# Four products of a Down step summed in one PSUM bank, with shared Mix banks and the Down weights' sums in Up block 1

## The chip, the cores and the metric

The kernel runs on one core of a Trainium2 chip. The metric is the device time of one execution, in microseconds (us). PE is the matmul engine (TensorE), DVE is VectorE, ACT is ScalarE, POOL is GpSimd, and SP issues the DMAs.

## What is computed

One encoder layer, applied with the same weights to two requests, 2048 and 1024 positions of 1024 channels. Both sub-layers have a residual sum around them:

```python
def _token_mixer(h, w_in, sgu_norm, w_spatial, b_spatial, w_out):
    z = h @ w_in                                     # 1024 x 1536
    f = fft2(z[..., :512] by groups of 128).real     # over positions x group channels
    zs = gelu(z[..., 512:]); u, v = zs[..., :512], zs[..., 512:]
    v = rmsnorm(v by heads of 128) * sgu_norm
    g = u * (w_spatial @ v in chunks of 128 positions + b_spatial)
    return concat([f, g]) @ w_out                    # 1024 x 1024

def _channel_mixer(h, w_up, conv_w, conv_b, w_down):
    a = conv3(h @ w_up) + conv_b                     # 1024 x 5632
    return (gelu(a[..., :2816]) * a[..., 2816:]) @ w_down

x = x + rmsnorm(_token_mixer(rmsnorm(x)));  x = x + rmsnorm(_channel_mixer(rmsnorm(x)))
```

## The kernel before

All data is fp32. An operand of a matmul is split into a rounded high part and the rest (`split`: a cast on ACT, then a subtraction on DVE, for some operands on POOL), and a product is high x high + high x low + low x high, three matmuls of 128x128 by 128x512 for each 128 rows of depth.

The large products go by Strassen-Winograd steps (`Step`): a 2x2 block product with seven products in place of eight. B11, B21, T4, T2, T3, T1, B22 are the numbers 0 to 6 of the products, and p0 to p6 are their PSUM banks, w0 to w6 their split left operands. `Step.sums` makes the four sums s1 to s4 of the left operand on POOL (s0 to s3 in the trace), `prep` splits one operand, `mm` runs the matmuls of one product into one bank, and `post` adds the bank to what the step has so far. In Down, `post` builds c11, c12, c21 and c22 from the seven banks in the half tiles u, c11, c21, c22, and `cadd` then adds these four to the partial result c that an earlier pass left in memory; `cload` fetches it and `cstore2` writes it back. A few steps at the end (`closing`) add straight into c.

The program is a sequence: Fourier, Gate (12 steps), Fourier again, Mix (12 mixes), Up in three blocks of 1024 positions (22 steps each, with the convolution in `centre` and `taps`, and the gate product in `gate`, on POOL), and Down in three passes q0, q1, q2 over the depth (12 steps each). Between stages `turnover` loads and splits the next right operands.

The order is written by hand: `at(slot, order, fn)` puts a call into a slot, and the slots are emitted in turn. A slot is one product. Each engine runs its instructions in the order emitted, and so does SP with the DMAs. `LEAD` says how many slots ahead of its product an operand is split (3 in Up, 2 elsewhere), and the second argument of `steps` how many slots ahead the sums stand. Pools: 43 tiles of 4 KB (`U`), 12 of 2 KB (`H`), 8 PSUM banks.

The right operand of Down needs sums of the weights too. `wd_load`, `wd_sums` and `wd_store` (four loads, four sums on POOL, four stores for each pair of blocks, eleven pairs) make them in the Gate stage and leave them in memory.

A mix makes rows of the mirrored halves: es (even) comes from one product, o (odd) from another, in two banks each; `odd_out` copies o to os on ACT, then POOL makes ds = es + os (L807) and es = es - os (L808). `direct` adds a product to ds from the d banks, `mirrored` one to es from the m banks (L887).

## Time and profile before

| | us |
|---|---|
| median of three runs | 2787.15 (2786.34 to 2789.84) |
| profiled execution | 2785.41 |
| its span | 2783.6 |
| PE busy | 2658.9 |
| DVE busy | 2254.6 |
| POOL busy | 1345.2 |
| ACT busy | 1192.9 |

The granted TensorE clock over the span is 0.987 of full speed. The stages start in the trace at: Gate 98.9, second Fourier 340, Mix 436, Up block 0 772.3, block 1 1236.3, block 2 1668.9, Down q0 2096.7, q1 2279.9, q2 2525.4; the last matmuls of Down are at 2766. A row of the timeline gives the start, the duration and, in square brackets, how long the engine had been idle and what ended that.

### The profile page before, as it was taken

Reading aid. Unit: us, or ns where it says so; the run is one execution under the profiler, and the core shown is the slowest. Engines: PE = TensorE matmul, PEld = TensorE weight load, DVE = VectorE, ACT = ScalarE, POOL = GpSimd, SP = SyncE. Lnnn points to the kernel's source line nnn. Section 1 sums busy time; section 2 is a strip of 40 time slices with the busy share of each in tenths; the row PEclk is TensorE's granted clock in tenths of the full one; section 3 lists DMA queues with packets and bytes.
Section 4 is the critical chain, followed back from the end, with each engine's and each line's share of the span. In section 5 each row is a group of like instructions: output and inputs, shape, how many; then the busy total and the mean of one; then the engine's idle time right before and its main releaser. Section 6 shows DMA issues by size and latency. Waiting matters only on the chain. (4 is left out here: it accounts for less than half of the span.)

```text
span 2783.6 us, 35169 instructions
## 1 busy us (share of the span) xinstructions
PE 2658.9 (96%) x11930; PEld 2161.3 (78%) x11930; DVE 2254.6 (81%) x3296; ACT 1192.9 (43%) x2273; POOL 1345.2 (48%) x866
## 2 busy tenths in 40 slices
PE   8899999999979999999999999999998999999997
PEld 7678887887757777777888887888886877887775
DVE  6788866767898888889887888888888677669998
ACT  5445534565544444454444444444443242214332
POOL 3856612548765545553122233212224356668787
PEclk9999999999999999999999999999999999999999
DMA  9446567667953454553443364344353465466665
GB/s 349 157 161 204 206 229 254 201 200 238 298 197 123 154 186 148 172 206 122 136 136 119 120 215 121 112 136 130 114 197 114 126 219 172 156 201 212 210 209 199
DMA packets 323924, 498.08 MB, mean 179 GB/s; under 512 B 27232, under 2 KB 176224, under 8 KB 323744
## 3 DMA queue, kind: packets, MB, share of 16 engines
q1 hardware_dynamic: 323744, 495.85, 54.0%
q8 instruction: 93, 1.52, 0.2%
q14 instruction: 87, 0.71, 0.1%
HBM read 337.42 MB, written 158.35 MB: 178 GB/s over the span
## 5 line engine op out<-in xcount | busy, mean ns | idle before, releaser
L1192 POOL TENSOR_TENSOR t0u<-t0u,t1u 128x1024 f32<-128x1024 f32 x66 | 178.7, 2710 | 410.9 <-ACT t0u L1191 232.5
L201 PE MATMUL p3u<-sox,w3u 128*128 128x512 f32 x792 | 197.4, 396 | 9.7 <-DVE w3u L101 6.6
L201 PE MATMUL p5u<-sox,w5u 128*128 128x512 f32 x792 | 193.4, 393 | 8.4 <-DVE w5u L101 8.4
L201 PE MATMUL p1u<-sox,w1u 128*128 128x512 f32 x792 | 194.6, 394 | 4.7 <-DVE w1u L101 3.4
L201 PE MATMUL p0u<-sox,w0u 128*128 128x512 f32 x792 | 191.8, 391 | 6.1 <-DVE w0u L101 5.7
L201 PE MATMUL p6u<-sox,w6u 128*128 128x512 f32 x792 | 192.8, 391 | 3.4 <-DVE w6u L101 3.4
L201 PE MATMUL p2u<-sox,w2u 128*128 128x512 f32 x792 | 193.1, 391 | 1.9 <-DVE w2u L101 1.7
L201 PE MATMUL p4u<-sox,w4u 128*128 128x512 f32 x792 | 190.5, 390 | 2.0 <-POOL w4u L101 1.9
L201 PEld LDWEIGHTS p3u<-sox,w3u 128*128 128x128 f32 x792 | 148.0, 190 | 48.9 <-DVE w3u L101 12.5
L201 PEld LDWEIGHTS p5u<-sox,w5u 128*128 128x128 f32 x792 | 148.8, 189 | 43.3 <-DVE w5u L101 12.4
L201 PEld LDWEIGHTS p1u<-sox,w1u 128*128 128x128 f32 x792 | 148.6, 189 | 41.2 <-DVE w1u L101 8.6
L201 PEld LDWEIGHTS p0u<-sox,w0u 128*128 128x128 f32 x792 | 148.0, 188 | 40.2 <-DVE w0u L101 9.0
L201 PEld LDWEIGHTS p6u<-sox,w6u 128*128 128x128 f32 x792 | 147.4, 188 | 39.0 <-DVE w6u L101 8.6
L201 PEld LDWEIGHTS p2u<-sox,w2u 128*128 128x128 f32 x792 | 147.6, 188 | 37.8 <-DVE w2u L101 7.5
L201 PEld LDWEIGHTS p4u<-sox,w4u 128*128 128x128 f32 x792 | 148.2, 188 | 35.1 <-POOL w4u L101 3.2
L1143 ACT ACTIVATE t1u<-p2u,cbt,cwt 128x512 f32<-128x512 f32 x66 | 51.5, 780 | 286.2 <-DVE p2u L1131 286.2
L209 ACT COPY ud<-p0d 128x512 f32<-128x512 f32 x34 | 20.0, 588 | 344.1 <-PE p0d L201 344.1
L1191 ACT ACTIVATE t0u<-t0u 128x1024 f32<-128x1024 f32 x66 | 70.1, 1062 | 201.9 <-DVE t0u L1155 138.9
L1143 ACT ACTIVATE t0u<-p1u,cbt,cwt 128x512 f32<-128x512 f32 x66 | 51.5, 781 | 234.5 <-DVE p1u L1137 234.5
L101 POOL TENSOR_TENSOR w4u<-a4u,w4u 128x512 fp32r<-128x512 f32 x44 | 56.9, 1295 | 192.3 <-ACT w4u L100 174.6
L1155 DVE SCALAR_TENSOR_TENSOR t0u<-p6u,cwt,t0u 128x511 f32<-128x511 f32 (+4 forms) x220 | 111.7, 533 | 6.0 <-ACT t0u L1143 2.0
L1155 DVE SCALAR_TENSOR_TENSOR t1u<-p2u,cwt,t1u 128x511 f32<-128x511 f32 (+4 forms) x220 | 111.7, 533 | 3.1
(363 smaller groups left out, 7268.5 us busy)
## 6 DMA issues: line engine op xcount, KB each, us to landing
g_d<-t0u SPq DMA_DIRECT2D x66, 512.0 KB, 2.9
srx<-xo_d SPq DMA_DIRECT2D x42, 512.0 KB, 6.3
xT<-xT SPq DMA_DIRECT2D x24, 512.0 KB, 8.5
xc<-xc SPq DMA_DIRECT2D x24, 512.0 KB, 5.5
zz<-z_d SPq DMA_DIRECT2D x48, 256.0 KB, 6.1
xr<-x_po SPq DMA_DIRECT2D x24, 512.0 KB, 5.5
xo_d<-hT SPq DMA_DIRECT2D x48, 256.0 KB, 4.0
ra0d<-g_d SPq DMA_DIRECT2D x24, 512.0 KB, 6.7
```

What stands on the lines that cost most here:

```text
L101: (eng or vec).tensor_tensor(l, src, h.bitcast(F32), op=ALU.subtract)
L201: nc.tensor.matmul(ps, lhsT=w[:, a, k], rhs=op[k][:, b], start=k == 0 and a + b == 0, stop=k == n - 1 and a == 1)
L209: nc.scalar.copy(self.u, p[0])
L1143: nc.scalar.activation(t[:, i], p, AF.Identity, bias=cbt[:, ti : ti + 1], scale=cwt[:, ti, 1:2])
L1155: vec.scalar_tensor_tensor(d, a, w, d, op0=ALU.mult, op1=ALU.add)
L1191: nc.scalar.activation(ga, ga, AF.Gelu_apprx_tanh)
L1192: nc.gpsimd.tensor_tensor(ga, ga, self.t[1], op=ALU.mult)
```

## The change

Down: the products go in the order B11, B21, T2, T1, T3, B22, T4. B11, T2, T3 and T4 run into one bank, each on top of what is there, and after each of them the bank is added to its quarter of c as it stands (in q0, where there is no c yet, it is copied by ACT). B21, T1 and B22 have banks of their own and are added too; T1's is added twice. The tile u and `cadd` are gone. c is loaded two slots ahead of the step; the sums stand three slots ahead. The weights' sum for T4 has the opposite sign.

Mix: odd and direct run into the same two banks. `odd_out` makes es - o on DVE straight from PSUM, and what was es becomes ds, to which the bank with odd and direct together is added after direct.

The weights' sums of Down, with their loads and stores, stand in Up block 1, one pair per step. In Up block 0 the operands are split two slots ahead (three as before in the other blocks), the sums stand three slots ahead, and the first two steps load one slot later. H has 14 tiles.

```diff
-    H = ctx.enter_context(tc.tile_pool(name="h", bufs=12))
+    H = ctx.enter_context(tc.tile_pool(name="h", bufs=14))
...
         def mm(self, j):
-            ps = self.p[j] = bank(f"p{j}{self.nm}")
+            chained = j in self.CHAIN[1:]
+            ps = self.p[j] = self.p[self.CHAIN[0]] if chained else bank(f"p{j}{self.nm}")
             w, op, n = self.w.pop(j), self.stage.op[j], self.n
             for k in range(n):
                 for a, b in ((0, 0), (0, 1), (1, 0)):
                     nc.tensor.matmul(
-                        ps, lhsT=w[:, a, k], rhs=op[k][:, b], start=k == 0 and a + b == 0, stop=k == n - 1 and a == 1
+                        ps, lhsT=w[:, a, k], rhs=op[k][:, b], start=k == 0 and a + b == 0 and not chained,
+                        stop=k == n - 1 and a == 1, skip_group_check=j in self.CHAIN,
                     )
...
     def wd_sums(i):
         t1 = half(f"wt{i}")
         bs = raws["wd", i]
-        right_sums(t1, *bs)
+        right_sums(t1, *bs, False)
+        nc.gpsimd.tensor_tensor(bs[2], bs[2], bs[0], op=ALU.subtract)
         bs.append(t1)
...
-    for i in range(NFT // 2):
-        at(SB + 7 * i + 1, LOAD, wd_load, i)
-        at(SB + 7 * i + 3, PREP, wd_sums, i)
-        at(SB + 7 * i + 7, STORE, wd_store, i)
...
         def odd_out(self):
-            os = unit(f"os{self.nm}", F32, (128, 2, 512))
-            self.ds = unit(f"ds{self.nm}", F32, (128, 2, 512))
+            self.ds = self.es
+            self.es = unit(f"em{self.nm}", F32, (128, 2, 512))
             for c in range(2):
-                nc.scalar.copy(os[:, c], self.o[c])
-            nc.gpsimd.tensor_tensor(self.ds, self.es, os, op=ALU.add)
-            nc.gpsimd.tensor_tensor(self.es, self.es, os, op=ALU.subtract)
+                vec.tensor_sub(self.es[:, c], self.ds[:, c], self.o[c])
...
         def direct(self):
-            self.m = [bank(f"d{c}{self.nm}") for c in range(2)]
-            product(*self.m, self.g[0], WG)
+            product(*self.o, self.g[0], WG, first=False, chain=True)
 
         def direct_out(self):
             for c in range(2):
-                vec.tensor_add(self.ds[:, c], self.ds[:, c], self.m[c])
+                vec.tensor_add(self.ds[:, c], self.ds[:, c], self.o[c])
...
     class Up(Step):
...
-        LEAD = 3
...
+            self.LEAD = 3 if blk else 2
...
+        if blk == 1:
+            for i in range(NFT // 2):
+                at(s + 7 * i + 22, LOAD, wd_load, i)
+                at(s + 7 * i + 25, PREP, wd_sums, i)
+                at(s + 7 * i + 29, STORE, wd_store, i)
...
-                at(u.s0 - 3, LOAD, u.load)
-                at(u.s0 - 3, PREP - 0.2, u.sums)
+                at(u.s0 - 2, LOAD, u.load)
+                at(u.s0 - 2, PREP - 0.2, u.sums)
                 products(u)
             elif blk == 0:
-                steps(u, 4)
+                steps(u, 3)
...
     class Down(Step):
+        ORDER = (B11, B21, T2, T1, T3, B22, T4)
+        CHAIN = (B11, T2, T3, T4)
...
         def cstore(self):
...
-                    nc.sync.dma_start(c_d[2 * self.tp + i, :, h], self.quads(i)[h])
+                    nc.sync.dma_start(c_d[2 * self.tp + i, :, h], self.c[i][h])
...
-        def cadd(self, i):
-            for h in range(2):
-                eng = vec if i == 0 and self.q == 2 else nc.gpsimd
-                eng.tensor_tensor(self.c[i][:, h], self.c[i][:, h], self.quads(i)[h], op=ALU.add)
-
         def post(self, j):
-
-            if not self.closing:
-                return super().post(j)
             p, add = self.p, vec.tensor_add
...
+            new = {B11: 0, T2: 1, T3: 3, T4: 2}.get(j)
+            if j == B11 and self.q == 0:
+                self.c = [[None, None], [None, None]]
+            if self.q == 0 and new is not None:
+                self.c[new // 2][new % 2] = half(f"c{new}{self.nm}")
+                nc.scalar.copy(self.c[new // 2][new % 2], p[j])
+            (c11, c12), (c21, c22) = self.c if self.q == 0 else ((c[:, 0], c[:, 1]) for c in self.c)
+            if self.q or new is None:
+                c = {B11: c11, B21: c11, T2: c12, T1: c12, B22: c12, T3: c22, T4: c21}[j]
+                add(c, c, p[j])
+            if j == T3:
+                add(c22, c22, p[T1])
...
-        turnover(s, stage, *(() if q else (range(7), 10, 14)))
+        turnover(s, stage, Down.ORDER, *(() if q else (10, 14)))
...
-            steps(d)
+            steps(d, 3)
...
-            at(s if d.closing else s + 3, LOAD, d.cload)
-            if not d.closing:
-                at(s + 6, OUT + 0.2, d.cadd, 1)
-                at(s + 7, OUT + 0.2, d.cadd, 0)
+            at(s - 2, LOAD, d.cload)
             if q == 1:
+                at(s + 8, STORE, d.cstore2, 0)
                 at(s + 8, STORE, d.cstore2, 1)
-                at(s + 9, STORE, d.cstore2, 0)
...
-                at(s + 4, OUT + 0.1, d.square, 1, 0)
-                at(s + 5, OUT + 0.1, d.square, 1, 1)
-                at(s + 6, OUT + 0.1, d.square, 0, 1)
+                at(s + 4, OUT + 0.1, d.square, 1, 1)
+                at(s + 5, OUT + 0.1, d.square, 0, 1)
+                at(s + 6, OUT + 0.1, d.square, 1, 0)
```

Where the rows of the order below have names such as s0g5 or w4u0_12, the digits behind the letter are the step (g5 is Gate step 5; u0_12 is Up block 0, step 12; d1_6 is Down q1, step 6).

POOL in the Gate stage, before, from step 4's last sum to step 5's first; wt and wd are the weights' sums, rvg the reciprocal root for the norm:

```order
L183 TENSOR_TENSOR s3g4_1554<-ra0g4_1431,s1g4_1552 128x512
L93 TENSOR_SCALAR rvg3_v_1639<-vsg3_1472 128x8
L94 TENSOR_TENSOR rvg3_y_1640<-rvg3_v_1639,power_84 128x8
L126 TENSOR_TENSOR wt4_1727<-wd41_1652,wd40_1651 128x512
L127 TENSOR_TENSOR wd41_1652<-wd43_1654,wd41_1652 128x512
L128 TENSOR_TENSOR wd40_1651<-wd41_1652,wd40_1651 128x512
L130 TENSOR_TENSOR wd42_1653<-wd40_1651,wd42_1653 128x512
L180 TENSOR_TENSOR s0g5_1767<-ra1g5_1648 128x512
```

and after:

```order
L184 TENSOR_TENSOR s3g4_1490<-ra0g4_1380,s1g4_1488 128x512
L93 TENSOR_SCALAR rvg3_v_1575<-vsg3_1413 128x8
L94 TENSOR_TENSOR rvg3_y_1576<-rvg3_v_1575,power_84 128x8
L181 TENSOR_TENSOR s0g5_1686<-ra1g5_1580 128x512
L182 TENSOR_TENSOR s1g5_1687<-s0g5_1686,ra0g5_1579 128x512
```

The four operations on wt and wd no longer stand between the root and s0 of the next step.

ACT in Up block 0, before, between the centres of step 11 and the casts of step 12:

```order
L1143 ACTIVATE t1u0_11_9234<-p2u0_11_9220,cbt_83,cwt_82 128x512
L1143 ACTIVATE t1u0_11_9234<-p5u0_11_9200,cbt_83,cwt_82 128x512
L1145 COPY halo_99<-p5u0_11_9200 128x1
L100 CAST w3u0_12_9240<-s1u0_12_9190 128x512
L100 CAST w4u0_12_9260<-s2u0_12_9191 128x512
L1143 ACTIVATE t0u0_11_9277<-p1u0_11_9263,cbt_83,cwt_82 128x512
L1143 ACTIVATE t0u0_11_9277<-p6u0_11_9243,cbt_83,cwt_82 128x512
L1145 COPY halo_99<-p6u0_11_9243 128x1
L100 CAST w5u0_12_9284<-s0u0_12_9189 128x512
```

and after:

```order
L1141 ACTIVATE t1u0_11_8984<-p2u0_11_8970,cbt_83,cwt_82 128x512
L1141 ACTIVATE t1u0_11_8984<-p5u0_11_8942,cbt_83,cwt_82 128x512
L1143 COPY halo_99<-p5u0_11_8942 128x1
L100 CAST w0u0_12_8990<-ra0u0_12_8892 128x512
L100 CAST w3u0_12_9010<-s1u0_12_8960 128x512
L1141 ACTIVATE t0u0_11_9027<-p1u0_11_9013,cbt_83,cwt_82 128x512
L1141 ACTIVATE t0u0_11_9027<-p6u0_11_8993,cbt_83,cwt_82 128x512
L1143 COPY halo_99<-p6u0_11_8993 128x1
L100 CAST w4u0_12_9034<-s2u0_12_8961 128x512
```

The cast of w4 moved from ahead of the centre of p1u to behind it, and the cast of w0 stands ahead of w3's.

DVE in Down q1, step 6, before:

```order
L101 TENSOR_TENSOR w3d1_6_20947<-s1d1_6_20877,w3d1_6_20947 128x512
L212 TENSOR_TENSOR c11d1_6_20963<-ud1_6_20939,p1d1_6_20950 128x512
L101 TENSOR_TENSOR w4d1_6_20966<-s2d1_6_20878,w4d1_6_20966 128x512
L101 TENSOR_TENSOR w5d1_6_20987<-s0d1_6_20876,w5d1_6_20987 128x512
L214 TENSOR_TENSOR ud1_6_20939<-ud1_6_20939,p3d1_6_20990 128x512
L101 TENSOR_TENSOR w6d1_6_21004<-s3d1_6_20879,w6d1_6_21004 128x512
L217 TENSOR_TENSOR c21d1_6_21020<-ud1_6_20939,p4d1_6_21007 128x512
L101 TENSOR_TENSOR w0d1_7_21030<-ra0d1_7_20943,w0d1_7_21030 128x512
L220 TENSOR_TENSOR c22d1_6_21046<-c21d1_6_21020,p5d1_6_21033 128x512
L221 TENSOR_TENSOR c21d1_6_21020<-c21d1_6_21020,p2d1_6_20969 128x512
L222 TENSOR_TENSOR ud1_6_20939<-ud1_6_20939,p5d1_6_21033 128x512
L101 TENSOR_TENSOR w1d1_7_21050<-ra0d1_7_20943,w1d1_7_21050 128x512
```

and after:

```order
L101 TENSOR_TENSOR w3d1_6_20767<-s1d1_6_20706,w3d1_6_20767 128x512
L1307 TENSOR_TENSOR c0d1_6_20730<-c0d1_6_20730,p0d1_6_20770 128x512
L101 TENSOR_TENSOR w5d1_6_20788<-s0d1_6_20705,w5d1_6_20788 128x512
L1307 TENSOR_TENSOR c0d1_6_20730<-c0d1_6_20730,p1d1_6_20791 128x512
L101 TENSOR_TENSOR w4d1_6_20807<-s2d1_6_20707,w4d1_6_20807 128x512
L1307 TENSOR_TENSOR c0d1_6_20730<-c0d1_6_20730,p0d1_6_20770 128x512
L101 TENSOR_TENSOR w6d1_6_20823<-s3d1_6_20708,w6d1_6_20823 128x512
L1307 TENSOR_TENSOR c0d1_6_20730<-c0d1_6_20730,p5d1_6_20826 128x512
L101 TENSOR_TENSOR w2d1_6_20848<-ra1d1_6_20650,w2d1_6_20848 128x512
L1307 TENSOR_TENSOR c1d1_6_20732<-c1d1_6_20732,p0d1_6_20770 128x512
L1309 TENSOR_TENSOR c1d1_6_20732<-c1d1_6_20732,p5d1_6_20826 128x512
```

Each step's additions all read a bank, and three of them name p0, the bank that four products share; the additions into u, c21 and c22 are gone.

## Rows read from the trace of the kernel before

**Rows 1.** The page's busy line: engine, us, share of the span, instructions.

```profile
PE 2658.9 (96%) x11930; PEld 2161.3 (78%) x11930; DVE 2254.6 (81%) x3296; ACT 1192.9 (43%) x2273; POOL 1345.2 (48%) x866
```

**Rows 2.** Busy time by stage: stretch, length, each engine's us, PEclk, DMA share, GB/s.

```profile
98.90:340.00 241.10, 226.12 (x1065) 186.33 (x1064) 198.50 (x287) 119.62 (x323) 155.90 (x120) 0.98 0.56 189
436.00:772.30 336.30, 319.96 (x1702) 268.52 (x1702) 239.12 (x302) 185.60 (x366) 192.32 (x116) 0.97 0.72 231
772.30:1236.30 464.00, 440.66 (x1873) 346.01 (x1872) 396.68 (x542) 207.55 (x395) 257.53 (x167) 0.99 0.51 169
1236.30:1668.90 432.60, 425.40 (x1861) 347.99 (x1860) 364.54 (x654) 191.65 (x316) 113.06 (x59) 1.00 0.43 140
1668.90:2096.70 427.80, 421.98 (x1838) 344.59 (x1836) 375.47 (x731) 191.00 (x314) 107.94 (x59) 1.00 0.42 136
2279.90:2525.40 245.50, 237.80 (x1030) 194.81 (x1029) 178.70 (x191) 69.35 (x132) 170.21 (x111) 0.99 0.59 192
2525.40:2766.00 240.60, 229.61 (x977) 182.20 (x977) 229.75 (x217) 80.73 (x147) 197.06 (x123) 0.99 0.63 202
```

**Rows 3.** Timeline of Up block 1, PE and POOL: start, us, engine, line, operation.

```profile
1418.33 2.88 PE L201 MATMUL p0u<-sox,w0u 128*128 128x512 f32 x12
...
1423.77 2.88 PE L201 MATMUL p4u<-sox,w4u 128*128 128x512 f32 x12
1417.24 1.29 POOL L101 TENSOR_TENSOR w4u<-a4u,w4u 128x512 fp32r<-128x512 f32 x1 [3.80 <-ACT w4u L100]
```

**Rows 4.** Timeline of a Gate step, POOL and DVE.

```profile
190.45 1.29 POOL L126 TENSOR_TENSOR wt<-wd,wd 128x512 f32<-128x512 f32 x1 [0.41 <-DMA wd<-wd]
...
196.47 1.34 POOL L180 TENSOR_TENSOR s0g<-ra1g 128x512 f32<-128x512 f32 x1
195.97 5.71 DVE L449 SCALAR_TENSOR_TENSOR v2g<-v2g,rvg_y,gsg 128x128 f32<-128x128 f32 x8
201.60 0.68 DVE L101 TENSOR_TENSOR w4g<-s2g,w4g 128x512 fp32r<-128x512 f32 x1
```

**Rows 5.** The norm's line in the Gate stage: duration in ns, min/median/max.

```profile
L449 DVE SCALAR_TENSOR_TENSOR v2g<-v2g,rvg_y,gsg x79: 336/341/1454, 126.5 to 339.9; 128x128 f32<-128x128 f32 x79
```

**Rows 6.** Groups, POOL in Down q1, then DVE in q2: xcount | busy us, mean ns.

```profile
L1290 POOL TENSOR_TENSOR c1d<-c1d,c22d 128x512 f32<-128x512 f32 x8 | 13.9, 1739 | 0.0
...
L1290 DVE TENSOR_TENSOR c0d<-c0d,c11d 128x512 f32<-128x512 f32 x9 | 16.0, 1775 | 0.0
```

**Rows 7.** Groups of the Mix stage, POOL and DVE.

```profile
L807 POOL TENSOR_TENSOR ds<-es,os 128x1024 f32<-128x1024 f32 x12 | 34.7, 2895 | 46.4 <-ACT os L806 43.7 <-ACT xr L911 2.0 <-issue 0.7
...
L808 POOL TENSOR_TENSOR es<-es,os 128x1024 f32<-128x1024 f32 x11 | 27.3, 2481 | 0.9
...
L887 DVE TENSOR_TENSOR es<-es,m 128x512 f32<-128x512 f32 x22 | 14.1, 681 | 8.1 <-POOL es L808 8.1
```

**Rows 8.** Groups of the Gate stage, POOL: the costliest of the weights' sums.

```profile
L127 POOL TENSOR_TENSOR wd<-wd,wd 128x512 f32<-128x512 f32 x11 | 19.1, 1733 | 0.9
```

**Rows 9.** Waits of PE, Gate stage: us in total, times, longest.

```profile
PE p4g L201 <- DVE w4g L101: 10.5, 10, 2.1
PE p4g L201 <- ACT w4g L100: 2.4, 1, 2.4
```

**Rows 10.** Waits of PE, Mix stage.

```profile
PE x L666 <- DVE ds L879: 5.9, 3, 3.0
PE pq L756 <- DVE tl L101: 4.2, 3, 3.3
PE pq L756 <- DVE ehl L101: 2.3, 1, 2.3
```

**Rows 11.** Timeline of a step of Up block 0: PE, DVE, ACT.

```profile
1112.55 2.88 PE L201 MATMUL p1u<-sox,w1u 128*128 128x512 f32 x12
1119.41 0.68 DVE L1137 TENSOR_TENSOR p1u<-uu,p1u 128x512 f32<-128x512 f32 x1
1120.13 0.78 ACT L1143 ACTIVATE t0u<-p1u,cbt,cwt 128x512 f32<-128x512 f32 x1 [2.89 <-DVE p1u L1137]
```

More of the change, by code (lines that the diff above doesn't have):

```diff
@@ L165, in tile_trunk @@
         LEAD = 2
+        CHAIN = ()
         def __init__(self, stage, nm):
@@ L656, in w4_split, with product @@
         W4.append(h)
-    def product(o0, o1, aparts, wparts, first=True, last=True):
+    def product(o0, o1, aparts, wparts, first=True, last=True, chain=False):
         n_last = len(aparts) - 1
@@ L665, in product @@
                 for c, o in ((0, o0), (1, o1)):
-                    nc.tensor.matmul(o, lhsT=a, rhs=w[:n, c * 512 : (c + 1) * 512], start=st, stop=sp)
+                    nc.tensor.matmul(
+                        o, lhsT=a, rhs=w[:n, c * 512 : (c + 1) * 512], start=st, stop=sp, skip_group_check=chain
+                    )
     OFFS = (0, 128, 260, 384)
@@ L799, in odd @@
             self.o = [bank(f"o{c}{self.nm}") for c in range(2)]
-            product(*self.o, self.Q, WQ)
+            product(*self.o, self.Q, WQ, chain=True)
         def odd_out(self):
-            os = unit(f"os{self.nm}", F32, (128, 2, 512))
-            self.ds = unit(f"ds{self.nm}", F32, (128, 2, 512))
+            self.ds = self.es
+            self.es = unit(f"em{self.nm}", F32, (128, 2, 512))
             for c in range(2):
-                nc.scalar.copy(os[:, c], self.o[c])
-            nc.gpsimd.tensor_tensor(self.ds, self.es, os, op=ALU.add)
-            nc.gpsimd.tensor_tensor(self.es, self.es, os, op=ALU.subtract)
+                vec.tensor_sub(self.es[:, c], self.ds[:, c], self.o[c])
             if self.special:
@@ L1285, in cload @@
                 self.c.append(c)
-        def cadd(self, i):
-            for h in range(2):
-                eng = vec if i == 0 and self.q == 2 else nc.gpsimd
-                eng.tensor_tensor(self.c[i][:, h], self.c[i][:, h], self.quads(i)[h], op=ALU.add)
         def post(self, j):
-            if not self.closing:
-                return super().post(j)
             p, add = self.p, vec.tensor_add
-            (c11, c12), (c21, c22) = ((c[:, 0], c[:, 1]) for c in self.c)
-            if j == 0:
-                self.u = half(f"u{self.nm}")
-                nc.scalar.copy(self.u, p[0])
-            elif j == 1:
-                add(c11, c11, p[1])
-                nc.gpsimd.tensor_tensor(c11, c11, self.u, op=ALU.add)
-            elif j == 2:
-                vec.tensor_sub(c21, c21, p[2])
-            elif j == 3:
-                add(self.u, self.u, p[3])
-                add(c12, c12, self.u)
-            elif j == 4:
-                add(self.u, self.u, p[4])
-                add(c21, c21, self.u)
-                add(c22, c22, self.u)
-            elif j == 5:
-                add(c22, c22, p[5])
-                add(c12, c12, p[5])
-            elif j == 6:
-                add(c12, c12, p[6])
+            new = {B11: 0, T2: 1, T3: 3, T4: 2}.get(j)
[10 more added lines that the diff above has]
+                add(c22, c22, p[T1])
         def cstore2(self, i):
```

## The prediction

> **What bounds the kernel now.** I read the page's busy line first, then the busy times by stage, then in each stage the waits of PE, and for each wait the timeline around one occurrence. The page [rows 1] has PE busy for 2658.9 us, 96% of the span. Since the change keeps every matmul, only PE's gaps can be won. The stages [rows 2] say where these lie. Products follow each other every 2.72 us (two of them from 1418.33 to 1423.77 in [rows 3]), so a step of seven takes 19.05 us. Up block 2 is 22 steps, 419 us at that pace, and takes 427.8; block 0 has as many steps and takes 464.0, 36 us more. Down q1 and q2 are 12 steps each, 228.6 us, and take 245.5 and 240.6. The Gate stage leaves PE idle for 241.1 - 226.1 = 15.0 us, the Mix stage for 336.3 - 320.0 = 16.3. What PE waits for is nearly always an operand that DVE splits; the question is who makes DVE late.
>
> One behaviour decides that. A 128x512 subtraction with both operands in SBUF takes DVE 0.68 us when POOL rests (w4g at 201.60 in [rows 4]), and the norm's 128x128 operation 0.341 us at the median [rows 5]; but the eight that start at 195.97 take 5.71 us beside POOL's sums, twice 8 x 0.341 [rows 4]. In Down q2 the sum of c11 into c0, two SBUF operands again, has a mean of 1.78 us [rows 6]. Operations that read PSUM stay at 0.68 (L887 in [rows 7]). So POOL's work costs DVE time, and where DVE is at its limit, PE time. The Trainium skill ("SBUF — State Buffer", section "Who interferes with whom") gives a reason: a DVE instruction with two SBUF inputs shares a read port with GpSimd, and whoever issues first shuts the other out. These rows agree.
>
> **Gate: the weights' sums leave.** In each of eleven steps POOL does four of them (four groups of eleven, the costliest with a mean of 1733 ns, [rows 8]) ahead of the step's own s0 to s3. In the step shown they hold POOL from 190.45 to 196.47; s0 to s2 then fall on the norm at 195.97, which ends near 201.6, and only then is w4g split [rows 4]. PE waits for that split 10.5 us in ten steps, and 2.4 for its cast [rows 9]. Without them s0 can start 6 us earlier and is past the norm's start; the norm shrinks by 5.71 - 2.73 = 3.0 us, three times the mean wait of 1.05. I take both rows, **-13**. At the small end the step's sums collide instead with the splits of w2g and w3g, and half is left, -7; at the large end all 15.0 of idle goes and the clock of 0.98 rises too, -18.
>
> **Mix: odd and direct share banks.** Removed are 24 ACT copies and two POOL operations of 1024 columns a mix, 34.7 and 27.3 us in all; added are 24 DVE subtractions from PSUM at L887's 0.68 us, 16.3 us [rows 7]. DVE gets back the 8.1 us in which L887 waited for POOL's es (L808), and is without POOL beside it for 62 us more. It is busy 239 of 336 us [rows 2], so it has room. PE's waits on DVE here are 5.9 + 4.2 + 2.3 = 12.4 us [rows 10], and that is the term, **-12**. Ends: -4 if the new subtractions stand just ahead of those splits, and -24 if all 16.3 of idle goes and most of what the clock's 0.97 costs. The o banks are held longer, through direct, and the d banks are free in return.
>
> **Up block 0: casts two products ahead, not three; sums three, not four.** In ACT's order w4's cast now stands behind the centre of p1u. The chain to the operand is then: DVE's operation on p1u 0.68 us, two centres of 0.78 on ACT, the cast (taken at a centre's price), and POOL's subtraction of 1.29 [rows 3, 11]: 4.3 us, with two products, 5.44, to do it in. 1.1 us are to spare if DVE takes p1u at once. In the step shown it doesn't: p1u's matmuls end at 1112.55 + 2.88 = 1115.43, DVE takes it at 1119.41 and ACT follows at 1120.13 [rows 11]. But that delay came in good part from the old order, in which w3's split waited behind the centre of p2u; with w0's cast ahead of w3's there DVE has other work. For the twenty steady steps I take **0**: +16 if 0.8 us a step of that delay is left, -10 if over half of what these steps lose now goes (of the 36 us against block 2 I give them 17, about half, and the start the rest). The start of the block, where the first pair's loads come a product later and POOL does less Mix work beside them, is **-1**, plus or minus 4.
>
> **Up block 1: the weights' sums arrive.** Each step gets 6 us of POOL (190.45 to 196.47, [rows 4]) in a stage where POOL is busy 113 of 432.6 us [rows 2]. They can delay w4u's subtraction, which ends at 1417.24 + 1.29 = 1418.53 and is needed at 1423.77 [rows 3]: 5.2 us hide most of it. DVE has 432.6 - 364.5 = 68 us idle in 22 steps, 3 a step, and loses about 1 of it beside the sums. I take **+2**, range 0 to +8. The eight transfers a step go to a stage where DMA is busy 0.43 of the time, from one where it is 0.56, and stand in SP's queue ahead of operand loads that are issued six products before their use; nothing for them.
>
> **Down: four products in one bank, results added from PSUM.** A step of q1 loses four POOL additions (1.74 us for c22, [rows 6]), one of q2 two on POOL and two on DVE, 1.78 and, by the uncontended price, 0.68. DVE's posts go from seven to eight, +0.68, each with an operand in PSUM, which contention doesn't lengthen. For DVE in q2 that is -1.8 us a step, where it is busy 229.8 of 240.6 us, the tightest of [rows 2]; in q1 it is the contention of four POOL additions less. The two stages stand 17 + 12 = 29 us over their steps; I take a third, **-9** (turnovers -5, steady q2 -3, closing -1). Large end two thirds, -18; small end +6, where the chain costs. The chain is a new wait: T2, T3 and T4 write a bank that DVE must have read since the chain's last product, with one other product, 2.72 us, between. Behind that addition in DVE's row stands the split that the next product needs anyway, so where DVE is late the wait adds one addition, 0.68 us, at most. The c loads are issued five products earlier, ahead of later operand loads on SP, and cover themselves.
>
> **The sum**, against the profiled execution's 2785.41 us: -13 - 12 - 1 + 0 + 2 - 9 = -33, 2752.4. The median of the runs stands 1.7 us above that execution, so the forecast is 2754.
>
> **Rivals.** 1, the other side: block 0's shorter lead. If DVE goes on taking p1u 4 us late, w4 comes 4.3 + 4.0 - 5.4 = 2.9 us late in each of 20 steps: 58 us, less the 17 lost there now, +41, giving 2795. It turns the result from 2.5 us a step on ((33 + 17) / 20); at half the delay it gives 2766. For it speaks the row at 1119.41, against it the new order of the casts and DVE's 464 - 397 = 67 idle us. 2, Mix gives nothing, because the 24 subtractions fall where DVE splits for PE: 2766. 3, the chain: in q2 DVE is so late that each step of q1 and q2 waits for the bank twice, 0.5 us each, over 24 steps +24, with the -9 kept: 2778. The Trainium skill speaks against reading a bank in use ("PSUM — Partial Sum Buffer", section "Summary: rules for kernel authors": while a result is read, matmuls should go to a different bank); here they do, through B21, T1 and B22 in between, and PE stands only if the read outlasts a product. No row of before shows such a wait. 4, the sums spoil block 1, w4u 1 us late in eleven steps: +11 in place of +2, 2763.
>
> **How the numbers follow.** Forecast 0.60; rival 1 0.16, half of it slower than before; rival 2 0.11; rival 3 0.08; rival 4 0.05. About 0.2%, 5.6 us, is what a measurement can tell from no change. Slower: 0.08 of rival 1, 0.02 of rival 3, 0.01 of several small ends together, 0.11. Same: 0.03 of rival 1 and 0.03 of rival 3, 0.06. Faster: 0.83. Below the forecast the terms' ends lie 5, 12, 4, 10, 2 and 9 us off, as independent errors 19; above it 6, 8, 4, 16, 6 and 15, 25. For 8 in 10 I go to 2728 below, and above to 2787, which takes in rivals 2, 3, 4 and the lower half of 1.
>
> **What would show it.** Right: in the Gate stage PE's waits for w4g sum to under 3 us; in Mix its waits for ds and tl are gone; POOL in q1 is down by some 70 us, and DVE in q2 by some 20; block 0 stays within 10 us of 464. Wrong: PE waiting for w4u or w3u in block 0 over 1 us a step; PE's waits in Down ended by DVE's additions into c (the chain); block 1 over 437 us with PE waiting for w4u.

## The result

The changed kernel takes 2759.05 us (2757.78 to 2759.55, four runs) where the kernel before takes 2788.24 in four runs: a ratio of 0.9895, 95% interval 0.9878 to 0.9912. The forecast was 2754, in a range of 2728 to 2787. The total is right; the terms of block 0 and block 1 lie outside their ranges, and Mix gave half of its term.

The page's busy line of the changed kernel, which answers to [rows 1], and its busy times by stage, which answer to [rows 2] (the same stages in the same order: Gate, Mix, Up block 0, 1 and 2, Down q1, q2):

```profile
PE 2650.9 (96%) x11930; PEld 2164.6 (78%) x11930; DVE 2156.4 (78%) x3282; ACT 1199.7 (44%) x2261; POOL 1172.1 (43%) x772
```

```profile
100.50:324.90 224.40, 221.64 (x1064) 186.15 (x1065) 164.59 (x289) 119.35 (x324) 91.63 (x76) 0.98 0.31 99
...
421.40:752.25 330.85, 317.92 (x1703) 267.51 (x1701) 244.51 (x330) 173.38 (x342) 134.54 (x95) 0.97 0.74 241
752.25:1205.55 453.30, 433.72 (x1873) 349.53 (x1872) 375.15 (x543) 207.76 (x395) 258.46 (x164) 0.98 0.52 172
1205.55:1653.40 447.85, 434.20 (x1861) 344.74 (x1859) 390.03 (x650) 191.73 (x316) 176.83 (x102) 1.00 0.56 185
1653.40:2085.05 431.65, 420.79 (x1837) 343.35 (x1837) 379.25 (x738) 191.01 (x314) 110.08 (x60) 1.00 0.41 133
...
2266.90:2514.80 247.90, 239.67 (x1029) 196.26 (x1030) 172.90 (x201) 71.82 (x123) 104.16 (x68) 0.97 0.57 190
2514.80:2742.00 227.20, 223.69 (x977) 184.09 (x977) 189.64 (x203) 75.57 (x130) 144.42 (x94) 0.99 0.65 209
```

Both programs issue the same 11930 matmuls, so the start of the n-th matmul in one trace can be set against the n-th in the other. The differences over a stage, in us, with the stage bounded by times of the kernel before:

| stretch | forecast | measured |
|---|---|---|
| Gate, 98.9 to 340 | -13 | -15.8 |
| second Fourier, 340 to 436 | 0 | +1.5 |
| Mix, 436 to 772.3 | -12 | -5.8 |
| block 0, start, to 840 | -1 | -0.9 |
| block 0, steady, to 1236.3 | 0 | -10.6 |
| block 1 with its turnover, to 1668.9 | +2 | +16.3 |
| block 2 and Down q0, to 2279.9 | 0 | 0.0 |
| Down q1, then q2, to 2766 | -9 | +3.4, -11.8 |
| last matmul | -33 | -24.1 |

The stretch before 98.9 gives another -0.5, and -1.9 behind the last matmul makes up the span's -26.0. Block 1 is 14 us worse than the sum had it, Mix 6 worse, block 0 11 better, the Gate stage 3 better.

**Block 1.** The steps with sums take 20.7 to 20.8 us between equal matmuls (ten of the eleven; the first takes 19.5), and the first without them is back at 19.04. A step of the changed kernel, PE, DVE and POOL:

```profile
1416.56 2.56 PE L203 MATMUL p3u<-sox,w3u 128*128 128x512 f32 x10 [0.50 <-DVE w3u L101]
...
1414.75 1.75 DVE L101 TENSOR_TENSOR w3u<-a3u,w3u 128x512 fp32r<-128x512 f32 x1 [2.08 <-ACT w3u L100]
...
1428.27 2.76 DVE L101 TENSOR_TENSOR w1u<-a1u,w1u 128x512 fp32r<-128x512 f32 x1
...
1414.66 1.30 POOL L694 TENSOR_TENSOR wd<-wd,wd 128x512 f32<-128x512 f32 x1
...
1428.09 2.40 POOL L1190 TENSOR_TENSOR t0u<-t0u,t1u 128x1024 f32<-128x1024 f32 x1 [10.43 <-ACT t0u L1189]
```

The split of w1u comes 0.18 us after the gate product has started on POOL and takes 2.76 us: until POOL's operation ends at 1430.49, and then another 0.54. The split of w3u comes 0.09 us after the start of the last weights' sum and takes 1.75 us, again until 0.54 behind the end of that operation (1415.96). How little DVE had to spare in the kernel before shows in the pace of its own steps; this split of w3u is followed by the next at 1435.01, 18.4 us later:

```profile
1416.62 0.69 DVE L101 TENSOR_TENSOR w3u<-a3u,w3u 128x512 fp32r<-128x512 f32 x1 [2.02 <-ACT w3u L100]
```

From 1320 to 1446 DVE keeps this pace there and never waits for PE, while a step of PE takes 19.04: the 0.6 us between the two are all its slack. (Once it has caught up, from 1448 on, it waits for PE.) The 2.02 us ahead of w3u are none: ACT's cast stands behind the centre of p2u, which stands behind DVE's own operation on p2u, so this gap moves with DVE. In that stretch the splits take 1.70 us (w0u) and 0.69 (w1u, w3u); in the changed kernel they take 0.68, 2.76 and 1.75, together 2.1 us more. DVE's step is 20.77 us there, 2.35 longer; less the slack of 0.62, that is the 1.73 us lost.

### The profile page after: what moved, and what is told of

The parts are those of the page before. It is cut to its first block, busy times and chain, and to the rows that moved or that the text cites. A ratio compares the mean times of both kernels' runs of the same rounds, so it can differ in the third digit from the quotient of the medians.

```text
span 2757.6 us, 35060 instructions
## 1 busy us (share of the span) xinstructions
PE 2650.9 (96%) x11930; PEld 2164.6 (78%) x11930; DVE 2156.4 (78%) x3282; ACT 1199.7 (44%) x2261; POOL 1172.1 (43%) x772
## 4 chain that ended last, share of the span: by engine, by line
PE 43%; DVE 7%; issue 3%; ACT 1%; DMA 1%; POOL 0%; SPq 0%; DVEq 0%; ACTq 0%; POOLq 0%
PE p0d L203 12%; PE p5u L203 4%; PE p4u L203 4%; PE p2u L203 4%; PE p3u L203 4%; PE p6d L203 3%; PE p0u L203 3%; PE p1d L203 3%; PE p5d L203 3%; PE p1u L203 3%; PE p6u L203 2%; DVE sow L156 1%; DVE w3u L101 1%; DVE t1u L1153 1%; DVE t0u L1153 1%
## 5 line engine op out<-in xcount | busy, mean ns | idle before, releaser
L203 PEld LDWEIGHTS p0u<-sox,w0u 128*128 128x128 f32 x792 | 149.1, 189 | 47.3 <-DVE w0u L101 16.3
L203 PEld LDWEIGHTS p6u<-sox,w6u 128*128 128x128 f32 x792 | 148.9, 188 | 33.9 <-DVE w6u L101 2.8
L181 POOL TENSOR_TENSOR s0d<-ra1d 128x512 f32<-128x512 f32 (+1 forms) x36 | 50.2, 1396 | 204.1 <-DMA ra1d<-g_d 190.1
L93 POOL TENSOR_SCALAR r_v<-ss 128x2 f32<-128x2 f32 (+1 forms) x38 | 15.9, 417 | 261.4 <-ACT scr L894 156.7
```

The source lines that it names most:

```text
L93: nc.gpsimd.tensor_scalar(v, ss, 1.0 / n, EPS, op0=ALU.mult, op1=ALU.add)
L181: nc.gpsimd.tensor_tensor(s1, a21, a22, op=ALU.add)
L203: nc.tensor.matmul(ps, lhsT=w[:, a, k], rhs=op[k][:, b], start=k == 0 and a + b == 0 and not chained, stop=k == n - 1 and a == 1, skip_gro ...
```

## The experiments

Where nothing else is said, an experiment is the changed kernel with one edit, and a difference over a stage is against the kernel before, as in the table. Medians are of four runs.

**e1, the sums back in the Gate stage.**

```diff
+    for i in range(NFT // 2):
+        at(SB + 7 * i + 1, LOAD, wd_load, i)
+        at(SB + 7 * i + 3, PREP, wd_sums, i)
+        at(SB + 7 * i + 7, STORE, wd_store, i)
...
-            for i in range(NFT // 2):
-                at(s + 7 * i + 22, LOAD, wd_load, i)
-                at(s + 7 * i + 25, PREP, wd_sums, i)
-                at(s + 7 * i + 29, STORE, wd_store, i)
```

> The changed kernel with the weights' sums, their loads and stores back in the Gate stage (everything else changed). Theory: in block 1 the four POOL sums lengthen DVE's splits of w1u (2.76 instead of 0.69 us) and w3u (1.75 instead of 0.69) by holding what both need, and the eleven steps with sums take 20.77 us instead of 19.04; without them block 1 has 19.04 in every step, -18.6 us there, and the Gate stage gets back its 14 to 16 us; total about 2756. Rival A, block 1's steps are long because of the eight extra transfers a step: the same -18.6, but then e2, which keeps the transfers, keeps the loss. Rival B, the Gate stage's gain came from something else in the change (H's 14 tiles): the Gate stage keeps its time and the total falls to about 2741.

2772.03 us, 13 slower than the changed kernel, ratio to before 0.9939 (0.9924 to 0.9953). Block 1 is at 0.0 from 1255 on, as expected; but the Gate stage (125 to 340) is not back at its old time, it is 18.4 us longer than before the change, with the same sums in the same slots. PE's waits for w4g there:

```profile
PE p4g L203 <- DVE w4g L101: 22.2, 10, 4.0
```

Twice the 10.5 of [rows 9]. The norm of the step that answers to [rows 4], and the last of POOL's sums:

```profile
203.71 6.62 DVE L452 SCALAR_TENSOR_TENSOR v2g<-v2g,rvg_y,gsg 128x128 f32<-128x128 f32 x8
...
208.07 1.33 POOL L184 TENSOR_TENSOR s3g<-ra0g,s1g 128x512 f32<-128x512 f32 x1
```

s3 now runs right behind s2 and on the norm, which takes 6.62 us instead of 5.71. The one other thing that has changed for POOL there is the pool of 2 KB tiles.

**e7, the same with 12 tiles of 2 KB.** e1 and:

```diff
-    H = ctx.enter_context(tc.tile_pool(name="h", bufs=14))
+    H = ctx.enter_context(tc.tile_pool(name="h", bufs=12))
```

> The changed kernel with the weights' sums back in the Gate stage, as in e1, and with 12 tiles of 2 KB instead of 14. Theory: with 12 tiles POOL's last sum, s3, has to wait for a tile until w4g is split, and so falls behind the norm instead of on it; the norm is back at 5.7 us from 6.6, PE's wait for w4g at some 10 us from 22, and the total falls from e1's 2772 to about 2754. Rival: the Gate stage's 32 us between e1 and the changed kernel come from the sums themselves, whatever the pool; then it stays at 2772.

2755.79 us. The Gate stage is 1.5 us off its old time, the wait for w4g is 10.0 us, and s3 waits for a tile until w4g has been split, as before the change:

```profile
204.54 1.61 POOL L184 TENSOR_TENSOR s3g<-ra0g,s1g 128x512 f32<-128x512 f32 x1 [1.95 <-DVE w4g L101]
```

Two more buffers let a sum run early, onto the norm, and cost 17 us. So the Gate term was right (moving the sums is worth 15.6 us there; e9 below, which has 12 tiles and no sums in the Gate stage, stands there at -14.1 like the changed kernel), and the whole move of the sums is worth -15.6 + 18.6 = +3: the changed kernel is 3 us slower than this one, within the scatter.

**e2, the sums behind w4u.**

```diff
-                at(s + 7 * i + 22, LOAD, wd_load, i)
-                at(s + 7 * i + 25, PREP, wd_sums, i)
-                at(s + 7 * i + 29, STORE, wd_store, i)
+                at(s + 7 * i + 27, LOAD, wd_load, i)
+                at(s + 7 * i + 30, PREP, wd_sums, i)
+                at(s + 7 * i + 34, STORE, wd_store, i)
```

> The changed kernel with the weights' sums of block 1 five slots later, so that on POOL they stand behind the subtraction of w4u and ahead of the next gate product instead of between the two. Theory (POOL beside the splits of w1u and w3u costs the time): POOL is idle for 10.4 us there, the splits of w1u and w3u go back to 0.69 us, at most w5u and w2u meet a sum; the eleven steps fall from 20.77 to 19.1 to 19.6 us, total 2743 to 2748. Rival A (the transfers) and a rival C (the sheer amount of POOL work a step): steps stay at 20.8 and the total at 2759.

2754.36 us; block 1 loses 9.2 us (1300 to 1530) instead of 17.7, and 1.9 instead of 0.9 from there to its end. About half of what was expected: w3u is back at 0.69 us, but the sums did not start behind w4u. They waited for a store to free their tiles and ran some 5 us later, ahead of the gate, where they met w1u, w0u, w5u and w6u in turn (means 1.65, 1.31, 0.93, 0.82 us; w0u had 1.47 before the change, beside the gate product). The transfers and the amount of POOL work are those of the changed kernel, so they alone don't make the loss; in e10, which keeps both, block 1 loses nothing.

**e3, the gate product of block 1 in halves.**

```diff
-            nc.gpsimd.tensor_tensor(ga, ga, self.t[1], op=ALU.mult)
+            for h in ((slice(0, 1), slice(1, 2)) if self.blk == 1 else (slice(0, 2),)):
+                nc.gpsimd.tensor_tensor(self.t[0][:, h], self.t[0][:, h], self.t[1][:, h], op=ALU.mult)
```

> The changed kernel with POOL's gate product of 1024 columns in block 1 made in two operations of 512 columns. Theory: DVE's split of w1u waits for the end of the POOL operation that is running when it comes, so with the gate in halves it takes about 1.4 us instead of 2.76; the eleven steps fall from 20.77 to about 19.5 us, total about 2745. Rival: what counts is how many us POOL is busy beside DVE, not how long one operation is; then w1u still takes about 2.7 us, since the sums follow, and the total stays at 2759.

2743.45 us, 0.9835 (0.9821 to 0.985). POOL does the same sums at the same place, and block 1 loses 4.4 us instead of 17.7. The groups of DVE's splits from 1330 to 1500, of the changed kernel and then of this one:

```profile
L101 DVE TENSOR_TENSOR w1u<-a1u,w1u 128x512 fp32r<-128x512 f32 x8 | 22.1, 2758 | 0.0
L101 DVE TENSOR_TENSOR w3u<-a3u,w3u 128x512 fp32r<-128x512 f32 x9 | 15.7, 1748 | 18.8 <-ACT w3u L100 18.8
```

```profile
L101 DVE TENSOR_TENSOR w3u<-a3u,w3u 128x512 fp32r<-128x512 f32 x8 | 14.0, 1750 | 16.7 <-ACT w3u L100 16.7
L101 DVE TENSOR_TENSOR w1u<-a1u,w1u 128x512 fp32r<-128x512 f32 x9 | 13.9, 1545 | 0.0
```

Only w1u changed, 2.76 to 1.55 us in the mean (1.65 in the steps with sums): it waits for the POOL operation that is under way, and that is now half as long. The Trainium skill ("SBUF — State Buffer", section "SBUF: two separate sides") has it that of a DVE operation with two SBUF inputs and a GpSimd operation that reads SBUF, the one that starts first keeps the shared pair of ports for the whole instruction, and the other is blocked. The rows agree: under **Block 1** POOL is first by 0.18 and 0.09 us, and the splits end 0.54 us behind it.

**e4, Up block 0 as before.**

```diff
-            self.LEAD = 3 if blk else 2
+            self.LEAD = 3
...
-                at(u.s0 - 2, LOAD, u.load)
-                at(u.s0 - 2, PREP - 0.2, u.sums)
+                at(u.s0 - 3, LOAD, u.load)
+                at(u.s0 - 3, PREP - 0.2, u.sums)
...
-                steps(u, 3)
+                steps(u, 4)
```

> The changed kernel with Up block 0 as before: operands split three slots ahead, sums four, first pair loaded at -3. Theory: the shorter lead gave the 10.6 us that steady block 0 is shorter; with it undone block 0 is back at some 20.0 us a step, total about 2769, and PE's waits there are again for w5u, w1u and w2u. Rival: the gain in block 0 comes from other parts of the change that last into it (the phase in which Mix hands over); then block 0 keeps its time and the total stays at 2759.

2761.37 us. Steady block 0 goes from -10.6 to -1.7 and its turnover from -2.3 to 0.0, so the shorter lead did give 11 us. But the start, which the theory had left alone, goes from -0.9 to -12.2. The shorter lead wins in the steady steps and loses the same at the start. Why steady steps gain, from the groups of DVE's splits over 17 steps, before and after:

```profile
L101 DVE TENSOR_TENSOR w1u<-ra0u,w1u 128x512 fp32r<-128x512 f32 x17 | 28.1, 1653 | 2.1 <-ACT w1u L100 2.1
L101 DVE TENSOR_TENSOR w2u<-ra1u,w2u 128x512 fp32r<-128x512 f32 x18 | 22.8, 1266 | 0.0
L101 DVE TENSOR_TENSOR w3u<-s1u,w3u 128x512 fp32r<-128x512 f32 x18 | 20.8, 1153 | 39.1 <-ACT w3u L100 39.1
```

```profile
L101 DVE TENSOR_TENSOR w1u<-ra0u,w1u 128x512 fp32r<-128x512 f32 x17 | 16.1, 946 | 0.6 <-ACT w1u L100 0.6
L101 DVE TENSOR_TENSOR w2u<-ra1u,w2u 128x512 fp32r<-128x512 f32 x18 | 14.3, 792 | 0.0
L101 DVE TENSOR_TENSOR w3u<-s1u,w3u 128x512 fp32r<-128x512 f32 x17 | 12.4, 727 | 0.6 <-ACT w3u L100 0.6
L101 DVE TENSOR_TENSOR w0u<-ra0u,w0u 128x512 fp32r<-128x512 f32 x17 | 20.3, 1194 | 38.1 <-ACT w0u L100 38.1
```

With the order moved by one product, POOL's work falls less on these three: 29 us of DVE time in 17 steps, at the same number of operations. By the starts in the traces it was not the sums alone. Before, eight of the w1u and four of the w3u began while POOL's gate product ran (means 2.74 and 2.77 us), and twelve of the w2u beside one of the sums (1.5 us); after, twelve of the w1u begin 0.1 to 0.9 us before the end of the gate product (mean 1.06), and only one of the w2u and w3u beside a sum. In e4 the old means are back (1601, 1266 and 1182 ns). DVE's wait for a cast did not go: the 39.1 us ahead of w3u stand ahead of w0u now, 38.1 in the last row.

**e6, Mix as before.**

```diff
...
             for c in range(2):
-                vec.tensor_sub(self.es[:, c], self.ds[:, c], self.o[c])
+                nc.scalar.copy(os[:, c], self.o[c])
+            nc.gpsimd.tensor_tensor(self.ds, self.es, os, op=ALU.add)
+            nc.gpsimd.tensor_tensor(self.es, self.es, os, op=ALU.subtract)
...
-            product(*self.o, self.g[0], WG, first=False, chain=True)
+            product(*self.m, self.g[0], WG)
```

> The changed kernel with the Mix stage as before (odd copied by ACT, sums of es and os on POOL, direct in banks of its own). Theory: the new Mix takes away only the waits for ds, about 4 us of 5.9; the waits for tl and ehl are made by POOL's residual additions of 1024 columns, which both have. Mix gets 4 to 8 us longer, total 2763 to 2767, with PE waiting for ds 5 to 6 us and for tl and ehl as before. Rival (the prediction's term): 12 us longer, total 2771.

2774.66 us: Mix is 18.0 us longer than in the changed kernel. Both expected numbers are too small. The old Mix in its new surroundings is 12.2 us longer than the same code was before the change: 5.5 of them from 757 on, and 5.8 from 652 to 665. The latter starts with one tie. The split of tl in the kernel before and POOL's L807, then the same two here (L808 is the same line):

```profile
660.35 0.68 DVE L101 TENSOR_TENSOR tl<-tr,th 128x512 fp32r<-128x512 f32 x1
...
660.46 2.82 POOL L807 TENSOR_TENSOR ds<-es,os 128x1024 f32<-128x1024 f32 x1 [0.58 <-ACT xr L911]
```

```profile
644.25 2.83 DVE L101 TENSOR_TENSOR tl<-tr,th 128x512 fp32r<-128x512 f32 x1
...
643.74 2.80 POOL L808 TENSOR_TENSOR ds<-es,os 128x1024 f32<-128x1024 f32 x1
```

Before, POOL had stood 0.58 us for ACT, and DVE was first by 0.11; here POOL did not stand and is first by 0.51, and the split takes 2.83 us instead of 0.68. PE, which had gained 1.4 us from 640 to 652 and so comes earlier, waits 3.98 us for this split instead of 0.42; its waits for tl in all of Mix go from 4.2 us [rows 10] to

```profile
PE pq L757 <- DVE tl L101: 7.9, 3, 4.0
```

That wait is 3.6 of the 5.8 us. The other 2.2 come behind it, where the granted clock is 0.50, the lower of its two levels (647 to 651 of this trace), and a matmul on tl takes 0.42 us; in the kernel before it was 1.00 at the same place (660 to 664), and the matmul took 0.28.

**e9, the old Mix, block 0 as before, and 12 tiles.** The edits of e6, e4 and of e7's one line together, the sums staying in block 1.

> e6 (Mix as before, the rest changed: 12.2 us longer in the Mix stage than before the change, with the same code there) with two more parts undone: Up block 0 as before, and 12 tiles of 2 KB instead of 14. Theory: those two parts cost the old Mix its 12 us, block 0's later start some 5 at the end (from 757 of before on), the 14 tiles some 6 around 650; with both undone the Mix stage has the time of before within 2 us, so that the Mix edit itself is worth 6 to 8. Rival A: only the end returns, -5, and the rest is phase. Rival B: nothing returns. Total by theory about 2764, by rival B 2776.

2807.76 us. Mix is 3.8 us longer than before the change, no longer 12.2. Its end (from 757) is back at 0.0 from +5.5. That part was block 0's later start: in e6 PE waits 4.3 us there for w0u, the operand of block 0's first product, and here it doesn't. The tiles, undone with it, are not the cause: e4, with 14 of them and block 0 as before, has no such wait either, where the changed kernel has 1.9 us. Of the 5.8 us around 652, 5.2 stay with 12 tiles as with 14, with POOL first by 0.51 us again: the tiles did not cause them, and rival A is right in the main. The total is far off for a reason that was not expected: block 1 is 44.9 us longer than before the change. PE's waits in block 1:

```profile
PE p6u L203 <- DVE w6u L101: 26.7, 11, 3.6
```

With 12 tiles the sums and block 1's own tiles don't both find room: in nine steps DVE's operation on vu, a tile of the same pool, waits for a store of the weights' sums to land, 33.9 us in all. The changed kernel, with 14, has no such wait.

**e5, Down as before.** The old class, its slots and the old sign of T4's sum in place of the new.

```diff
-        ORDER = (B11, B21, T2, T1, T3, B22, T4)
-        CHAIN = (B11, T2, T3, T4)
...
+        def cadd(self, i):
+            for h in range(2):
+                eng = vec if i == 0 and self.q == 2 else nc.gpsimd
+                eng.tensor_tensor(self.c[i][:, h], self.c[i][:, h], self.quads(i)[h], op=ALU.add)
...
+            if not d.closing:
+                at(s + 6, OUT + 0.2, d.cadd, 1)
+                at(s + 7, OUT + 0.2, d.cadd, 0)
```

> The changed kernel with Down as before the change (seven banks, partial results by POOL and DVE after the step). Theory: the new Down gives 10.3 us in q2, because DVE, full there, loses two additions of two SBUF operands and POOL's neighbours go; it gives nothing in steady q1 (19.04 us a step either way) and nothing at the two turnovers, where the chain waits for DVE. So q2 returns to some 19.85 us a step and a late closing, total about 2768, and q1 stays. Rival: q2 is faster because the sums and c loads stand earlier, with the turnover before it; the loss then shows in the first steps of q2 only.

2767.31 us. q2 from 2545 on goes from -10.3 to +1.1, and q1's steady steps are 19.04 us either way. The turnovers are within 4 us, with no gain from the change.

**e12, POOL's additions put back, without DVE's.** In q1 four and in q2 two additions a step on POOL, of a tile of zeros onto itself; `pads` is two of them, of 128x512.

```diff
+            if not d.closing:
+                at(s + 6, OUT + 0.2, pads)
+                if q == 1:
+                    at(s + 7, OUT + 0.2, pads)
```

> The changed kernel with POOL additions of 128x512 put back into Down that do no work (a tile of zeros onto itself), as many and in the slots where the additions of the partial results stood on POOL before: four a step in q1, two in q2. Theory: q2's 10 us came from the two additions that DVE itself lost, which lengthened under POOL; POOL's own two cost DVE at most 2 us a step, less than the 3 it now has to spare, so q2 stays at 19.04 a step and the total at 2759 to 2761. Rival: it was POOL's additions beside DVE; then q2 is back at 19.85 a step and the total at about 2768.

2762.33 us, and q2 keeps its -10.2. Busy times of 180 us of q2, before (2560 to 2740), after, and with the additions (both 2536 to 2716):

```profile
2560.00:2740.00 180.00, 178.24 (x768) 142.00 (x767) 170.22 (x163) 58.95 (x107) 145.35 (x90) 1.00 0.65 207
```

```profile
2536.00:2716.00 180.00, 180.00 (x796) 149.05 (x795) 146.89 (x159) 60.20 (x103) 111.81 (x73) 1.00 0.65 208
```

```profile
2536.00:2716.00 180.00, 180.00 (x796) 149.05 (x795) 147.74 (x161) 59.61 (x102) 136.39 (x92) 1.00 0.65 208
```

POOL is busy 25 us more, DVE 0.9 more, PE not less. So q2's gain does not come from there being fewer POOL operations; DVE's own two additions are left as its likely source, with what stood beside them. That is not shown in full: the pads wait for nothing, where the old additions waited for DVE, so they need not stand beside the same splits, and this run says nothing of their place.

**e8, three edits, read by stage.** The gate in halves in all blocks, block 0's first two steps at lead 3, and POOL's residual of Mix in halves, which is the edit shown:

```diff
-                nc.gpsimd.tensor_tensor(m, m, self.xr[i], op=ALU.add)
+                for c in range(2):
+                    h = slice(c * 512, c * 512 + 512)
+                    nc.gpsimd.tensor_tensor(m[:, h], m[:, h], self.xr[i][:, h], op=ALU.add)
```

> The changed kernel with three edits in three stages: POOL's residual additions in Mix in halves of 512 columns; Up block 0's first two steps as before the change (loads at -3, lead 3) and the others at lead 2; the gate product in halves in all blocks. Theory: Mix's waits for tl and ehl fall by half, -3; the start of block 0 loses the 11 us that e4 won there (from -0.9 to about -12 against before) while steady block 0 keeps its -10; block 1 as in e3, -13. Total about 2731. Rivals: the start's 11 us in e4 came from the lead of the later steps, then the start keeps its time; POOL's residual holds DVE as long in halves, then Mix keeps its time; 2743 if both.

2731.32 us, 0.9785 (0.9768 to 0.9801). The total is the expected one by luck: the start of block 0 gave 9 us less than expected, and Mix, steady block 0, block 1 and block 2 (-2.5) together gave that much more. Mix is at -10.2, against -4.9 to -8.6 in the runs with the Mix of the changed kernel; but PE's waits for tl and ehl did not fall by half, they are 3.7 and 3.4 us against 3.8 and 2.3, so the theory for Mix is not shown. Block 0's steady part is at -14.0; its start at -2.5, so the start's 11 us do not come from the lead of the first two steps: the rival holds.

**e10, five edits.** e8, with lead 3 and sums four ahead in the first four steps of block 0, the sums behind w4u as in e2, and Down's turnover preparation behind a slot's additions:

```diff
-            at(d, PREP + 0.1, stage.prep, j, (k,))
+            at(d, when, stage.prep, j, (k,))
...
-        turnover(s, stage, Down.ORDER, *(() if q else (10, 14)))
+        turnover(s, stage, Down.ORDER, *((6, 10) if q else (10, 14)), OUT + 0.05)
```

> e8 with: in Up block 0 the first four steps (not two) at lead 3 with sums four slots ahead; the weights' sums of block 1 behind w4u's subtraction, as in e2, beside the gate halves; and in Down's turnovers the preparation of the next stage's operands in a slot behind that slot's addition into c, not ahead of it. Theory: the start of block 0 gets e4's -12 (from -2.5 in e8); block 1's sums cost 1 to 3 us instead of 4.4; at the two turnovers PE waits for the chain's additions less, by one preparation of 1.75 us each, -2 to -4 in all. Total about 2716. Rival for the chain: the additions into c are late because of the splits and sums ahead of them; then the turnovers keep their time. Rival for the start: the gain of e4 needs lead 3 in all steps, then 2726.

2722.11 us, 0.9764 (0.9749 to 0.9779). Block 0's start is at -9.2 (more steps and the sums' place were changed together, so which of them did it stays open); block 1 from 1255 to 1668.9 at -0.7, so the weights' sums now cost nothing there. The two turnovers gain about 2 us against e8, not clear of the scatter. From 2230 to 2500 PE still waits 3.8 us for c0d, but most of that is no longer the chain's: at q1's first step w3d is split at 2241.60 and PE starts at 2242.35, 0.75 us later, where the changed kernel has 2.4.

**e11, the residual in quarters of 256 columns, on top of e10.**

```diff
-                for c in range(2):
-                    h = slice(c * 512, c * 512 + 512)
+                for c in range(4):
+                    h = slice(c * 256, c * 256 + 256)
```

> e10 with POOL's residual additions in Mix in quarters of 256 columns instead of halves. Theory: DVE's splits of ehl, gl and tl wait for the end of the POOL operation that is running, so shorter operations shorten PE's waits for tl and ehl in Mix from the 7 us of e8 to some 4; Mix -2, total 2720. Rival: POOL takes longer in more pieces and the waits move to where its results are needed (norm and xr); then Mix stays or grows by 2.

2720.91 us, 0.9758 (0.9744 to 0.9773): not to be told from e10. In Mix (-14.2 against -11.3) PE's waits on tl and ehl are 3.7 us against 4.8. With e10 it is the fastest, 38 us below the changed kernel.

## Why the prediction was right, and where it was wrong

**Gate, right.** -13 forecast, -15.8 measured. PE's waits for w4g are 0.4 us, from 10.5 [rows 9], and between e7 and the changed kernel the Gate stage's steady part differs by 15.6.

**Mix, the mechanism right, the term's size not.** The waits of the changed kernel, which answer to [rows 10]:

```profile
PE pq L757 <- DVE tl L101: 3.8, 3, 2.4
PE pq L757 <- DVE ehl L101: 2.3, 1, 2.3
PE x L669 <- DVE es L877: 1.9, 2, 1.2
```

The forecast counted all 12.4 us as going with L807 and L808. Only the wait for ds did (5.9 to 1.9). tl and ehl stand behind POOL's residual additions, which stay. In e8, e10 and e11 those are shorter and so is Mix, but the waits for tl and ehl fall only in e10 and e11 (4.8 and 3.7 us in all, from 6.1), not in e8 (7.1); how the shorter additions help is not shown in full. Undone in the new surroundings the edit costs 18 us, since the old code is itself 12 longer there: 5.5 at the end, by block 0's later start (e9 and e4), and 5.8 behind the tie at 652, in PE's wait and in the clock after it (e6). Why POOL no longer stands for ACT there wasn't followed further back.

**Block 0, wrong by 11 us.** The step that failed is "For the twenty steady steps I take 0". It looked at the one operand that the shorter lead makes late, w4u, and at p1u's delay. Rival 1 did not come: PE waits for w4u 3.1 us in five steps from 819 on. DVE now takes p1u 0.7 to 3.2 us behind its matmuls, where it was 4.0 to 6.1; a step of the changed kernel, PE and DVE:

```profile
1062.44 2.88 PE L203 MATMUL p1u<-sox,w1u 128*128 128x512 f32 x12
...
1068.53 0.69 DVE L1135 TENSOR_TENSOR p1u<-uu,p1u 128x512 f32<-128x512 f32 x1
```

So far the argument against the rival held; but the idle time ahead of w3u was not filled, it moved ahead of w0u (e4). (At half the delay the rival's own sum gives 4.3 + 2.0 - 5.4 = 0.9 us a step and 2755; its 2766 stands for half of the 2.9 us.) What the sum left out was where POOL's gate product and sums lie against three of DVE's splits. The start's -1 was right, and hid that the old lead would give -12 there (e4).

**Block 1, wrong by 14 us**, beyond the range given and beyond rival 4, which had named the place but the wrong operand (w4u, where PE waits 0.6 us in all). The step that failed: "DVE has 432.6 - 364.5 = 68 us idle in 22 steps, 3 a step, and loses about 1 of it beside the sums". Two of the three were DVE's wait for ACT's cast of w3u, behind DVE's own operation, and can't take up a delay; the slack was 0.6 us a step. And the loss was 2.3, because two splits came just behind the start of a POOL operation, one of them of 1024 columns.

**Down, right in sum, not in place.** -8.4 against -9. Steady q2 gave 10.3 with the closing instead of 4, and the turnovers cost 1.9 instead of giving 5: rival 3's chain wait is there, not in steady steps. PE waits at q1's first step and last:

```profile
PE p0d L203 <- DVE c0d L1307: 4.9, 1, 4.9
...
PE p0d L203 <- DVE c1d L1307: 2.3, 1, 2.3
```

There DVE prepares the next stage between the splits and the additions. The first of the two, DVE and PE:

```profile
2276.97 1.75 DVE L101 TENSOR_TENSOR w3d<-s1d,w3d 128x512 fp32r<-128x512 f32 x1
2278.65 1.74 DVE L156 TENSOR_TENSOR sow<-srw,sow 128x512 fp32r<-128x512 f32 x1
2280.32 0.67 DVE L1307 TENSOR_TENSOR c0d<-c0d,p0d 128x512 f32<-128x512 f32 x1
...
2281.14 4.95 PE L203 MATMUL p0d<-sow,w3d 128*128 128x512 f32 x12 [4.88 <-DVE c0d L1307]
```

w3d is split at 2278.72, and without the chain PE could start then; it starts 2.4 us later. So the step "where DVE is late the wait adds one addition, 0.68 us, at most" fails: a preparation of 1.74 us stands ahead of the addition. In steady steps no wait of PE for a c addition is in the trace.

The total held by luck: block 0 gave about what block 1 took, neither foreseen. Of the signs named for being right, POOL in q1 came (from 170.2 to 104.2 us) and so did the wait for w4g; the waits for tl did not go, DVE in q2 fell by 40 us where 20 were named, and block 0 is 10.7 us shorter, just outside its 10. Of the signs of being wrong, block 1 is at 447.9 us, over 437, but with PE waiting for w3u and w1u, not w4u.

## What to carry to other kernels

Before work is put on POOL, look which DVE operations with two SBUF operands will start just behind one of its operations: the price is the rest of that operation. Here shorter POOL operations and another order won what the sums had cost in block 1, with no less POOL work: halving one product won back 13 of 18 us (e3), and the order the rest (e10). Idle time of an engine that ends on its own result, through another engine, is not slack; compare the engine's own pace with that of the bottleneck, 18.4 against 19.04 us here. A stage's time under one edit can depend on who wins a tie of some tenths of a microsecond, so an edit should be undone in its new surroundings before it is called worth what its stage gained.

## What was not expected of the hardware

Two more buffers cost 17 us (e1 and e7), because a POOL sum that no longer waits for a tile runs onto DVE's norm. And the same two instructions, 0.11 us apart one way and 0.51 the other, differ by 2.15 us in DVE's time; and behind PE's longer wait for that split, 3.98 us, its granted clock was 0.50 where it had been 1.00 (e6).
